# A hybrid retention layer on one NeuronCore: the first stage's modulation vectors, sums and fill rearranged

## The chip, the cores and the metric

The kernel runs on one core of a Trainium2 chip. A core has five engines that each work through their own instructions in order: TensorE (matrix products; its loads of the stationary operand are counted apart), VectorE, ScalarE, GpSimd, and SyncE, which issues transfers. Transfers run on 16 DMA engines that all issuing queues share. The metric is the device time of one execution in microseconds (us), the median of several runs.

## The reference

The layer takes 512 latent tokens `x` and 256 context tokens `ctx` of width 1024. Nine modulation vectors per token group come from one conditioning vector:

```python
mods = split((silu(c) @ w_mod + b_mod), 9)            # for x: sh1, sc1, g1, sh2, ...
mods_c = split(silu(c_ctx) @ w_mod + b_mod, 9)        # for the context
modulate(x, w, shift, scale) = rmsnorm(x, w) * (1 + scale) + shift
swiglu(x, w_in, w_out): a, b = split(x @ w_in); return (silu(a) * b) @ w_out

h  = x   + 0.5 * g1  * swiglu(modulate(x,   norm_ffn1, sh1,  sc1),  w_ffn1_in, w_ffn1_out)
hc = ctx + 0.5 * g1c * swiglu(modulate(ctx, norm_ffn1, sh1c, sc1c), w_ffn1_in, w_ffn1_out)
# then: bidirectional retention beside a convolution branch, gates, a second SwiGLU, a final RMSNorm
```

Everything is float32. The change concerns only what is needed before and during the first two column pairs of `w_ffn1_in`.

## The kernel before

Activations lie transposed: eight blocks of 128 channels (`b` = 0 to 7), each with 512 latent columns and 256 context columns in one tile `hx[b]`. A float32 product is made of three matmuls of a faster format: each operand is split into a high and a low part, and `mm3` (lines 110 to 113) issues high x high, high x low, low x high. A weight unit is loaded (line 100), its high part made on ScalarE (line 102) and its low part on VectorE (line 104). `wh` and `wl` have four buffers each; a unit holds one column block of 128 for all eight `b`.

The first stage is `start` (line 515 on), called from `ffn1`:

- `x` is loaded block by block (line 518). ScalarE squares the blocks and VectorE sums them (lines 239 to 246). `rstd_sum` adds over the channels with two-column matmuls against ones (lines 255, 256), takes a root, and `rstd_bcast` spreads the result over all partitions with one matmul (line 269).
- At the very beginning the conditioning rows `cc` are loaded into zeroed tiles, put through Silu and spread over the partitions with matmuls (line 159); ScalarE copies them out of PSUM as `ccrow` (line 521).
- `first_mods(b)` (line 167) makes scale and shift of block `b` for the latent and the context tokens. It loads 512 KB of weights for the scale and 512 KB for the shift (line 173) into tiles that later hold other operands (`th`, `tl`). The scale is eight matmuls with the two columns of `cs` held in the array and 128 weight columns streaming (line 176); the two rows that come out are copied (line 179) and transposed (line 180). The shift is a sum over products: VectorE does it for the latent tokens (line 183), GpSimd multiplies and ScalarE sums for the context tokens (lines 186, 187). `shift` (lines 194, 195) adds the two half sums and the bias.
- `norm_start` (line 505 on) makes the block's modulated input: VectorE (line 510), ScalarE's high part (511), VectorE's low part (512), ScalarE's full value (513).
- `products(n, k1)` issues the products of the first pair of column blocks (`n` = 0, `px[0]` and `px[1]`) or the second (`n` = 1) over the blocks that are ready, for the 512 latent columns. After that come the context tokens' row sums and norms, and their products for the four weights one after the other into `pc`.

`plain` in `ffn1` then takes Silu of one half times the other. `operands` (line 362) forms sums of the inputs for a saving scheme of multiplication that `chunk` uses from the fifth pair on. The third and fourth pairs follow with no such scheme. Their results, and all later ones, are accumulated in `hdram`, a DRAM tensor that is filled with `x` and `ctx` (lines 562, 563) and to which `part_sum` adds by accumulating transfers from GpSimd's queue (line 600). `mods(n)` (line 197) makes the later modulation vectors on VectorE, from weights loaded on GpSimd's queue into two `wm` buffers (line 200).

Each engine's order is made when the program is built, by a planner that takes the instructions by their place in the source but lets one go ahead when those before it on its engine aren't due yet. So the fill, which stands at the end of `start`, is issued in the first microseconds, on GpSimd's queue. A tile's buffer is reused only when all readers of its former contents are done, and the instruction that reuses it waits on its own engine.

Of the kernel before, what the change touches and what calls it, by code (L numbers as in the profile page):

```python
# [16 lines left out]
P = 128  # L17
# [37 lines left out]


# [6 lines left out]
def hybrid_layer_kernel(ctx: ExitStack, tc: tile.TileContext, a: dict, out: bass.AP):  # L63
# [62 lines left out]
    nc.sync.dma_start(cs, a["ccT"])  # L126
# [38 lines left out]
    rtags = [f"{t}{i}" for i in range(8) for t in ("th", "tl")]  # L165

    def first_mods(b):


        raw = [[t_((P, 512), F32, rtags[(4 * b + 2 * i + n) % 16]) for n in range(2)] for i in range(2)]  # L170
        for i in range(2):
            for n in range(2):
                nc.sync.dma_start(raw[i][n], a["w_mod0"][2 * b + i, :, n * 512:(n + 1) * 512])
        pm = ps()
        for k in range(KT):
            nc.tensor.matmul(pm[0:2, 0:P], cs[:, k, :], raw[0][k // 4][:, k % 4 * P:(k % 4 + 1) * P],
                             start=k == 0, stop=k == KT - 1)
        row = tmp()
        nc.vector.tensor_copy(row[0:2, 0:P], pm[0:2, 0:P])
        nc.tensor.transpose(pm[:, P:P + 2], row[0:2, 0:P], ident[0:2, 0:2])  # L180
        for n in range(2):
            c = slice(n * 512, (n + 1) * 512)
            nc.vector.scalar_tensor_tensor(tmp((P, 512), BF16), raw[1][n], 1.0, ccrow[0][:, c], ALU.mult, ALU.mult,
                                           accum_out=dots[:, b, 0, n:n + 1])
# [3 lines left out]
        nc.vector.tensor_scalar(ab1[:, 0, b, :], pm[:, P:P + 2], bm1[:, 8 + b:9 + b], vec[:, V_N1 + b:V_N1 + b + 1],  # L188
                                ALU.add, ALU.mult)
        shift(slice(b, b + 1), 0)  # L190

    def shift(bs, v):
        t = ab1[:, 1, bs, v]
        nc.vector.tensor_add(t, dots[:, bs, v, 0], dots[:, bs, v, 1])
        nc.vector.tensor_add(t, t, vec[:, V_BM + bs.start:V_BM + bs.stop])
# [232 lines left out]
    def ffn1(u):  # L428
# [7 lines left out]
        def plain(pa, pb, pc):  # L436
            s = t_((P, LA), F32, "sg", 4)
            nc.scalar.activation(s[:, xs], pa, AF.Silu)
            nc.vector.tensor_mul(s[:, xs], s[:, xs], pb)
            nc.scalar.activation(s[:, cx], pc[:, 0, :], AF.Silu)  # L440
            nc.vector.tensor_mul(s[:, cx], s[:, cx], pc[:, 1, :])
            return s
# [7 lines left out]
        for gi, (k0, nk) in enumerate(GROUPS1):  # L450
            for j in range(2 if k0 == 0 else 0, nk):
# [10 lines left out]
                keep(j, plain(pa, pb, pc))  # L462
# [52 lines left out]
    def start(u, uc):  # L515
# [7 lines left out]
        r1 = r1c = None  # L523
# [8 lines left out]
        dg = rstd_sum(acc, sq, whole)  # L532
        for b in range(KT):
            first_mods(b)
            if b == 0:
                r1 = rstd_bcast(dg)
                w += units(a["w1i"][0])
            norm_start(b, xs, r1, deriv["x1"], *u[b])
            if b == 3:
                w += units(a["w1i"][1])  # L540
            if b == 5:
                for i in range(KT):
# [597 lines left out]
```

## Time and profile before

| what | us |
|---|---|
| median of three runs | 1779.79 |
| lowest and highest run | 1775.0 and 1780.79 |
| the profiled execution, its own time | 1775.92 |
| its span, first to last instruction | 1774.1 |
| TensorE busy | 1720.5 (97%) |
| VectorE busy | 1148.9 (65%) |
| ScalarE busy | 674.4 (38%) |
| GpSimd busy | 141.9 (8%) |

A row of the page's groups names line, engine, operation, output and inputs with their shapes, then the count, the busy time in us and the mean in ns. A row of the order of time begins with start and duration in us; what stands in brackets is the idle time before it and what ended it. A row of the windows gives a stretch, its length, the busy time of TensorE, its weight loads, VectorE, ScalarE and GpSimd, the granted TensorE clock as a share of full speed, the DMA share and GB/s. Matmuls overlap, so the distance between the starts of two matmuls is their price, not the duration in the row.

### The profile page before, as it was taken

How to read it: one execution, taken by the hardware profiler on the slowest of the kernel's cores; microseconds unless marked ns; L12 is line 12 of the kernel's file. 1: busy time of each engine (PE TensorE's matmuls, PEld its weight loads, DVE VectorE, ACT ScalarE, POOL GpSimd, SP SyncE). 2: the span in 40 equal slices, each digit the busy share in tenths (PEclk: the TensorE clock that was granted, in tenths of full speed). 3: DMA queues.
4: the chain of work that ended last, by engine and by line, in shares of the span. 5: the costliest groups of instructions: out<-in, count | busy, mean ns of one | idle time of the engine just before them, and what ended most of it. 6: DMA issues, size and time to landing. Idle time of an engine off the chain costs nothing. (4 is left out here: it accounts for less than half of the span.)

```text
span 1774.1 us, 22474 instructions
## 1 busy us (share of the span) xinstructions
PE 1720.5 (97%) x8918; PEld 1495.8 (84%) x8918; DVE 1148.9 (65%) x1808; ACT 674.4 (38%) x963; POOL 141.9 (8%) x221
## 2 busy tenths in 40 slices
PE   5999999999999889999999999999999999999997
PEld 3689999998989778888888888888888988888887
DVE  5895858785767788793886679293755643333335
ACT  4643434443344532342342334233563432222222
POOL 3401020202122000010000000001100000000000
PEclk7999999999999999999999999999999999999998
DMA  9347373848585221242142125115652133333221
GB/s 342 115 135 162 119 179 105 195 164 206 188 209 190 87 83 60 68 159 72 48 155 85 58 72 178 60 48 176 198 194 97 61 118 97 99 93 101 97 84 48
DMA packets 68253, 221.95 MB, mean 125 GB/s; under 512 B 8178, under 2 KB 9202, under 8 KB 68148
## 3 DMA queue, kind: packets, MB, share of 16 engines
q1 hardware_dynamic: 45652, 146.84, 25.4%
q0 software_dynamic: 21920, 72.64, 14.9%
q8 instruction: 69, 1.13, 0.3%
q10 hardware_dynamic: 576, 1.05, 0.2%
q14 instruction: 36, 0.29, 0.0%
HBM read 192.18 MB, written 31.46 MB: 126 GB/s over the span
## 5 line engine op out<-in xcount | busy, mean ns | idle before, releaser
L102 ACT CAST wh<-wraw 128x1024 fp32r<-128x1024 f32 (+2 forms) x212 | 219.5, 1037 | 555.7 <-PE ps L112 308.7
L104 DVE TENSOR_TENSOR wl<-wraw,wh 128x1024 fp32r<-128x1024 f32 (+2 forms) x212 | 254.4, 1203 | 194.8 <-ACT wh L102 190.3
L111 PE MATMUL ps<-uh,wh 128*128 128x512 f32 (+1 forms) x924 | 332.4, 361 | 1.5 <-ACT uh L292 1.1
L113 PE MATMUL ps<-uh,wl 128*128 128x512 f32 (+1 forms) x924 | 330.6, 359 | 0.8 <-DVE wl L104 0.8
L112 PE MATMUL ps<-ul,wh 128*128 128x512 f32 (+1 forms) x832 | 297.8, 359 | 0.2
L112 PE MATMUL ps<-gx,wh 128*128 128x512 f32 (+1 forms) x544 | 204.0, 377 | 0.0
L113 PE MATMUL ps<-gx,wl 128*128 128x512 f32 (+1 forms) x544 | 204.0, 377 | 0.0
L111 PE MATMUL ps<-gx,wh 128*128 128x512 f32 (+1 forms) x544 | 203.7, 377 | 0.2 <-ACT gx L300 0.2
L111 PEld LDWEIGHTS ps<-uh,wh 128*128 128x128 f32 x924 | 174.9, 190 | 28.4 <-ACT uh L292 1.5
L113 PEld LDWEIGHTS ps<-uh,wl 128*128 128x128 f32 x924 | 175.1, 190 | 26.7 <-DVE wl L104 1.3
L696 DVE SCALAR_TENSOR_TENSOR h<-y,vec,h 128x512 f32<-128x512 f32 x240 | 179.6, 749 | 5.5
L112 PEld LDWEIGHTS ps<-ul,wh 128*128 128x128 f32 x832 | 157.8, 190 | 23.8 <-issue 0.7
L111 PE MATMUL ps<-hx,wh 128*128 128x512 f32 (+1 forms) x364 | 121.5, 336 | 5.3 <-ACT hx L300 3.8
L112 PE MATMUL ps<-hx,wh 128*128 128x512 f32 (+1 forms) x364 | 121.7, 334 | 0.7 <-DVE hx L301 0.7
L113 PE MATMUL ps<-hx,wl 128*128 128x512 f32 (+1 forms) x364 | 121.1, 333 | 0.0
L111 PEld LDWEIGHTS ps<-gx,wh 128*128 128x128 f32 x544 | 102.1, 188 | 19.2 <-ACT gx L300 0.4
L113 PEld LDWEIGHTS ps<-gx,wl 128*128 128x128 f32 x544 | 102.0, 188 | 18.7
L112 PEld LDWEIGHTS ps<-gx,wh 128*128 128x128 f32 x544 | 102.0, 188 | 18.6
L359 DVE TENSOR_TENSOR wl<-wraw,wh 128x1024 fp32r<-128x1024 f32 x54 | 66.1, 1223 | 55.6 <-ACT wh L358 55.4
L404 PE MATMUL ps<-th,wl 128*128 128x384 f32 x288 | 96.2, 334 | 0.0
L404 PE MATMUL ps<-th,wh 128*128 128x384 f32 x288 | 96.2, 334 | 0.0
L404 PE MATMUL ps<-tl,wh 128*128 128x384 f32 x288 | 96.2, 334 | 0.0
(272 smaller groups left out, 3100.5 us busy)
## 6 DMA issues: line engine op xcount, KB each, us to landing
wm<-in_w_mod POOLq DMA_DIRECT2D x56, 512.0 KB, 4.4
wraw<-in_w1i SPq DMA_DIRECT2D x44, 512.0 KB, 6.0
wraw<-in_w2i SPq DMA_DIRECT2D x44, 512.0 KB, 3.7
hdram<-sg POOLq DMA_DIRECT2D x40, 384.0 KB, 7.4
wraw<-in_w1o SPq DMA_DIRECT2D x16, 512.0 KB, 3.6
wraw<-in_w_cv SPq DMA_DIRECT2D x16, 512.0 KB, 3.8
wraw<-in_w_v SPq DMA_DIRECT2D x16, 512.0 KB, 5.7
wraw<-in_w_rg SPq DMA_DIRECT2D x16, 512.0 KB, 3.8
```

The source lines that it names most:

```text
L102: nc.scalar.copy(hi, raw)
L104: nc.vector.tensor_sub(lo, raw, f32(hi))
L111: nc.tensor.matmul(o, w[0], x[0], start=first, stop=False)
L112: nc.tensor.matmul(o, w[0], x[1], start=False, stop=False)
L113: nc.tensor.matmul(o, w[1], x[0], start=False, stop=last)
L359: nc.vector.tensor_sub(lo, src, f32(hi))
L404: nc.tensor.matmul(o, w[i][:, ws], x[k][m], start=first and k == n == 0, stop=k == 3 and n == 2, skip_group_check=True)
L696: nc.vector.scalar_tensor_tensor(o, y[:, t:t + L], vec[:, w0 + t:w0 + t + 1], o, ALU.mult, ALU.add)
```

## The change

- **Loads of the conditioning vectors.** `cs` and `cc` are loaded from ScalarE's queue. The zeroed tiles and the matmul against a first row of ones are gone; the matmul now takes one partition of `ones` and of `crow`.
- **Weights of the first modulation.** `load_mods(b)` loads them one block ahead of `first_mods(b)`. The scale weights take two `sg` tiles, or one `wm` tile in blocks 2, 3, 6 and 7; the shift weights keep a tile pair of their own for every block.
- **Scales on TensorE, the other way round.** The 128x128 weight block is held in the array and the two columns of `cs` stream, so the result is already a column per token group: no copy, no transpose.
- **Shifts.** Blocks 0 to 3 (`PE_SHIFT`) compute them in the same way on TensorE, for both token groups. In blocks 4 to 7 VectorE sums over products, for the latent tokens in `first_mods` and for the context tokens later, from the kept weights. Nothing of this is left on GpSimd or ScalarE.
- **Order in `start`.** The weights of the second pair are loaded after block 1. Products run one block closer to the norms. The context tokens are loaded after the loop; their row sums come after all products of the latent tokens; Silu and gating of the first pair come before the context norms. The context products now run with the blocks outside and the four weights inside.
- **Fill of `hdram`.** It stands after `start`, on ScalarE's queue.

```diff
     cs = cp.tile([P, KT, 2], F32, name="cs")
-    nc.sync.dma_start(cs, a["ccT"])
+    nc.scalar.dma_start(cs, a["ccT"])
...
-        nc.vector.memset(crow[v], 0.0)
-        nc.sync.dma_start(crow[v][0:1, :], a["cc"][:, v * D:(v + 1) * D])
+        nc.scalar.dma_start(crow[v][0:1, :], a["cc"][:, v * D:(v + 1) * D])
...
-            nc.tensor.matmul(pb, first, crow[v][:, c], start=True, stop=True)
+            nc.tensor.matmul(pb, ones[0:1, :], crow[v][0:1, c], start=True, stop=True)
...
+    def load_mods(b):
+        for i in range(2):
+            if i == 0 and b % 4 >= 2:
+                raw = t_((P, D), F32, "wm", 2)
+                nc.sync.dma_start(raw, a["w_mod0"][2 * b])
+                parts = [raw[:, :512], raw[:, 512:]]
+            else:
+                parts = [t_((P, 512), F32, "sg", 4) if i == 0 else t_((P, 512), F32, rtags[2 * b + n]) for n in range(2)]
+                for n in range(2):
+                    nc.sync.dma_start(parts[n], a["w_mod0"][2 * b + i, :, n * 512:(n + 1) * 512])
+            shifts[b, i] = parts
+
     def first_mods(b):
         pm = ps()
-        for k in range(KT):
-            nc.tensor.matmul(pm[0:2, 0:P], cs[:, k, :], raw[0][k // 4][:, k % 4 * P:(k % 4 + 1) * P],
-                             start=k == 0, stop=k == KT - 1)
-        row = tmp()
-        nc.vector.tensor_copy(row[0:2, 0:P], pm[0:2, 0:P])
-        nc.tensor.transpose(pm[:, P:P + 2], row[0:2, 0:P], ident[0:2, 0:2])
+        for i in range(2 if b < PE_SHIFT else 1):
+            raw = shifts[b, i]
+            for k in range(KT):
+                nc.tensor.matmul(pm[:, 2 * i:2 * i + 2], raw[k // 4][:, k % 4 * P:(k % 4 + 1) * P], cs[:, k, :],
+                                 start=k == 0, stop=k == KT - 1)
+        nc.vector.tensor_scalar(ab1[:, 0, b, :], pm[:, 0:2], bm1[:, 8 + b:9 + b], vec[:, V_N1 + b:V_N1 + b + 1],
+                                ALU.add, ALU.mult)
+        if b < PE_SHIFT:
+            nc.vector.tensor_scalar_add(ab1[:, 1, b, :], pm[:, 2:4], vec[:, V_BM + b:V_BM + b + 1])
+        else:
+            shift(b, 0)
+
+    def shift(b, v):
         for n in range(2):
             c = slice(n * 512, (n + 1) * 512)
-            nc.vector.scalar_tensor_tensor(tmp((P, 512), BF16), raw[1][n], 1.0, ccrow[0][:, c], ALU.mult, ALU.mult,
-                                           accum_out=dots[:, b, 0, n:n + 1])
-            m = tmp()
-            nc.gpsimd.tensor_mul(m, raw[1][n], ccrow[1][:, c])
-            nc.scalar.activation(m, m, AF.Copy, accum_out=dots[:, b, 1, n:n + 1])
...
+            nc.vector.scalar_tensor_tensor(tmp((P, 512), BF16), shifts[b, 1][n], 1.0, ccrow[v][:, c], ALU.mult,
+                                           ALU.mult, accum_out=dots[:, b, v, n:n + 1])
+        nc.vector.tensor_scalar(ab1[:, 1, b, v:v + 1], dots[:, b, v, 0:1], dots[:, b, v, 1:2],
+                                vec[:, V_BM + b:V_BM + b + 1], ALU.add, ALU.add)
...
+        todo_g = start(ux, uc, gate)
+        nc.scalar.dma_start(hdram[:, :, xs], a["xT"])
+        nc.scalar.dma_start(hdram[:, :, cx], a["ctxT"])
...
         dg = rstd_sum(acc, sq, whole)
+        load_mods(0)
         for b in range(KT):
+            if b == 0:
+                w += units(a["w1i"][0])
+            if b + 1 < KT:
+                load_mods(b + 1)
             first_mods(b)
             if b == 0:
                 r1 = rstd_bcast(dg)
-                w += units(a["w1i"][0])
             norm_start(b, xs, r1, deriv["x1"], *u[b])
-            if b == 3:
+            if b == 1:
                 w += units(a["w1i"][1])
...
             if b >= 1:
-                products(0, b - 1)
-            if b >= 4:
-                products(1, b - 2)
+                products(0, b)
+            if b >= 3:
+                products(1, b - 1)
+        for i in range(KT):
+            nc.sync.dma_start(hx[i][:, cx], a["ctxT"][:, i, :])
         sqc = [square_sum(accc, hx[j][:, cx], j) for j in range(KT)][-1]
...
         products(0, KT)
         products(1, KT)
-        pc = [ps((P, 2, LC)) for _ in range(2)]
-        for i in range(4):
-            proj(pc[i // 2][:, i % 2, :], w[i], uc)
+        r1c = rstd_bcast(rstd_sum(accc, sqc, wholec))
+        s = [t_((P, LA), F32, "sg", 4) for _ in range(2)]
+        gate(s[0], xs, px[0], px[1])
+        pc = [ps()[:, :LC] for _ in range(4)]
+        for b in range(KT):
+            if b >= PE_SHIFT:
+                shift(b, 1)
+            norm_start(b, cx, r1c, deriv["c1"], *uc[b])
+            for i in range(4):
+                proj(pc[i], w[i], uc, (b,))
+        gate(s[1], xs, px[2], px[3])
+        for n in range(2):
+            gate(s[n], cx, pc[2 * n], pc[2 * n + 1])
         nc.gpsimd.dma_start(rope, a["rope"])
-        nc.gpsimd.dma_start(hdram[:, :, xs], a["xT"])
-        nc.gpsimd.dma_start(hdram[:, :, cx], a["ctxT"])
```

The host-side layout of the first modulation weights changes with it: scale weights and the shift weights of blocks 0 to 3 are laid out for the array, the shift weights of blocks 4 to 7 row by row for VectorE.

More of the change, by code (lines that the diff above doesn't have):

```diff
@@ L165, in hybrid_layer_kernel @@
     rtags = [f"{t}{i}" for i in range(8) for t in ("th", "tl")]
+    shifts = {}
+    def load_mods(b):
[9 more added lines that the diff above has]
+            shifts[b, i] = parts
@@ L187, in first_mods @@
-            nc.scalar.activation(m, m, AF.Copy, accum_out=dots[:, b, 1, n:n + 1])
[L188 to L195, printed above, removed]
+            nc.vector.scalar_tensor_tensor(tmp((P, 512), BF16), shifts[b, 1][n], 1.0, ccrow[v][:, c], ALU.mult,
+                                           ALU.mult, accum_out=dots[:, b, v, n:n + 1])
@@ L434, in keep, with gate @@
             g.append((hi, lo))
[L436 to L442, printed above, removed]
+        def gate(s, c, pa, pb):
+            nc.scalar.activation(s[:, c], pa, AF.Silu)
+            nc.vector.tensor_mul(s[:, c], s[:, c], pb)
         ux, uc = part(u, xs), part(u, cx)
-        todo_g = [plain(*p) for p in start(ux, uc)]
+        todo_g = start(ux, uc, gate)
+        nc.scalar.dma_start(hdram[:, :, xs], a["xT"])
+        nc.scalar.dma_start(hdram[:, :, cx], a["ctxT"])
         t = [operands(kb) for kb in range(4)]
@@ L461, in ffn1 @@
                 proj(pc[:, 1, :], wb, uc)
-                keep(j, plain(pa, pb, pc))
+                s = t_((P, LA), F32, "sg", 4)
+                gate(s, xs, pa, pb)
+                gate(s, cx, pc[:, 0, :], pc[:, 1, :])
+                keep(j, s)
             n = 2 * nk * P
@@ L513, in norm_start, with start @@
         nc.scalar.activation(src, v, AF.Identity, bias=sh)
-    def start(u, uc):
+    def start(u, uc, gate):
         for b in range(KT):
@@ L522, in start @@
         w, px = [], [ps() for _ in range(4)]
-        r1 = r1c = None
         done = [0, 0]
@@ L536, in start @@
                 r1 = rstd_bcast(dg)
[L537 removed]
             norm_start(b, xs, r1, deriv["x1"], *u[b])
[L539 removed]
+            if b == 1:
                 w += units(a["w1i"][1])
[L541 to L543 removed]
             if b >= 1:
[L545 to L555 removed]
+                products(0, b)
[3 more added lines that the diff above has]
+            nc.sync.dma_start(hx[i][:, cx], a["ctxT"][:, i, :])
+        sqc = [square_sum(accc, hx[j][:, cx], j) for j in range(KT)][-1]
         products(0, KT)
         products(1, KT)
[L558 to L560 removed]
+        r1c = rstd_bcast(rstd_sum(accc, sqc, wholec))
[11 more added lines that the diff above has]
+            gate(s[n], cx, pc[2 * n], pc[2 * n + 1])
         nc.gpsimd.dma_start(rope, a["rope"])
[L562 to L564 removed]
+        return s
     todo = list(range(len(MOD_STEPS)))
@@ L1084, in _layout @@
     wm = w_mod[0].T.reshape(9, 8, P, D)
-    wn = w_mod[0][:, D:2 * D].reshape(KT, P, 8, P).transpose(2, 1, 0, 3).reshape(8, P, -1)
+    wn = w_mod[0][:, :2 * D].reshape(KT, P, 2, 8, P).transpose(2, 3, 1, 0, 4).reshape(2, 8, P, -1)
     wi = w_in[0]
@@ L1101, in _layout @@
         "vecs": np.concatenate(vecs, axis=1),
-        "w_mod0": np.stack([w for b in range(8) for w in (wn[b], wm[0, b])]),
+        "w_mod0": np.stack([w for b in range(8) for w in (wn[1, b], wn[0, b] if b < PE_SHIFT else wm[0, b])]),
         "w_mod": np.stack([wm[i, b] for i, b in MOD_STEPS]),
```

17 lines of the change are left out of this document (1 added, 16 removed).

## The prediction

> **What bounds the kernel now.** I read the page's row of slices first, to see where TensorE lacks work or clock, then the busy times of four long stretches, then the order of time in the first 95 us.
>
> ```profile
> span 1774.1 us, 22474 instructions
> PEclk7999999999999999999999999999999999999998
> 27.60:95.00 67.40, 59.77 (x342) 43.55 (x343) 61.62 (x139) 41.21 (x87) 27.84 (x17) 0.93 0.50 174
> 95.00:160.00 65.00, 65.00 (x372) 57.00 (x371) 51.09 (x90) 25.40 (x37) 10.46 (x15) 1.00 0.63 166
> 82.40 0.40 PE L111 MATMUL ps<-uh,wh 128*128 128x256 f32 x2
> 94.99 0.40 PE L111 MATMUL ps<-uh,wh 128*128 128x512 f32 x1
> ```
>
> The windows give, in order, TensorE, its weight loads, VectorE, ScalarE, GpSimd, the granted clock, the DMA share and GB/s. From 95 us on TensorE has no gap (65.00 of 65.00) at full clock. The change touches only the stage before that. So its worth is the shift of one landmark, which I call J: the first product of the third column pair, at 94.99, when all products of the first two pairs are done (those of the context tokens begin at 82.40). Up to J, three things are close together: TensorE 59.77 busy of 67.40, VectorE 61.62, and DMA, whose share is about 1.0 in the early windows below. I take whichever is last in each stretch.
>
> ```profile
> 3.27 0.79 POOL L562 DMA_DIRECT2D hdram<-in_xT  x1
> hx<-in_xT SPq DMA_DIRECT2D x8, 256.0 KB, 9.3
> 4.30 0.63 ACT L239 ACTIVATE acc<-hx 128x512 f32<-128x512 f32 x1 [1.57 <-DMA hx<-in_xT]
> 22.77 0.69 DVE L243 TENSOR_TENSOR t<-hx 128x512 f32<-128x512 f32 x1 [3.53 <-DMA hx<-in_xT]
> 24.12 0.59 PE L255 MATMUL ps<-ones,acc 128*128 128x2 f32 x2 [12.32 <-DVE acc L246]
> 27.62 0.58 PE L176 MATMUL ps<-th,cs 128*2 128x128 f32 x2
> 30.97 1.12 PE L269 MATMUL ps<-t,ones 128*128 128x512 f32 x2
> ```
>
> The eight blocks of x land from 4.30 to 22.77, because the fill of `hdram`, issued at 3.27, and the first weights share the bus. The row sums (16 passes, 24.12 to 27.62) and the root follow. The broadcast, from 30.97 for 1.1 us, lets the blocks be normalised.
>
> **The clock.** The granted clock changes only at multiples of 3.41 us, so I cut windows there:
>
> ```profile
> 6.84:10.25 3.41, 3.41 (x5) 1.33 (x4) 0.83 (x2) 0.63 (x1) 0.00 (x0) 1.00 1.01 381
> 10.25:13.66 3.41, 1.55 (x4) 0.38 (x2) 0.69 (x1) 0.76 (x2) 0.00 (x0) 1.00 1.04 396
> 13.66:17.08 3.42, 0.00 (x0) 0.00 (x0) 1.39 (x2) 1.13 (x2) 0.00 (x0) 1.00 1.01 372
> 23.90:27.32 3.42, 3.20 (x15) 3.20 (x16) 0.16 (x1) 0.37 (x1) 0.00 (x0) 0.50 1.03 382
> 27.32:30.73 3.41, 3.41 (x17) 2.15 (x18) 2.49 (x11) 2.77 (x5) 1.78 (x2) 0.50 1.06 359
> 30.73:34.15 3.42, 3.42 (x25) 1.98 (x23) 3.08 (x5) 0.72 (x2) 1.25 (x1) 1.00 0.91 341
> 34.15:37.56 3.41, 1.24 (x12) 0.75 (x9) 3.41 (x6) 0.00 (x0) 3.16 (x2) 1.00 1.02 347
> 37.56:40.97 3.41, 2.12 (x7) 1.35 (x8) 3.41 (x10) 2.33 (x5) 0.68 (x2) 0.50 1.04 402
> 587.11:590.52 3.41, 1.95 (x15) 1.87 (x15) 3.41 (x8) 2.27 (x5) 0.54 (x1) 1.00 0.26 97
> 589.61 0.33 PE L256 MATMUL ps<-ones,t 128*128 128x2 f32 x2
> 590.52:593.93 3.41, 0.00 (x0) 0.00 (x0) 3.34 (x11) 1.77 (x3) 0.54 (x1) 0.50 0.56 180
> 593.93:597.35 3.42, 2.96 (x12) 2.78 (x13) 3.42 (x11) 2.14 (x6) 0.00 (x0) 0.50 0.77 235
> ```
>
> The window 23.90 to 27.32 is filled with two-column passes (3.20 of 3.42), and the clock stays at 0.50. The next is filled with 128-column passes, and the clock is released at its end. A window with 1.55 busy and no two-column pass keeps the clock (10.25). One with 1.95 busy, two-column passes alone from 589.61 on, loses it (590.52). One with 1.24 loses it too (37.56). So two-column passes seem to count as nearly idle. About 0.45 of a window (1.55 of 3.41) must stream to keep the clock, and a window with 2.96 of 3.42 releases it.
>
> **The change part by part.** Prices of passes, the first and the last row of runs at full clock, then two rows at half clock, then the other engines:
>
> ```profile
> 77.70 0.38 PE L255 MATMUL ps<-ones,accc 128*128 128x2 f32 x2
> 78.62 0.49 PE L112 MATMUL ps<-ul,wh 128*128 128x512 f32 x1
> 72.25 0.39 PE L112 MATMUL ps<-ul,wh 128*128 128x512 f32 x1
> 77.47 0.39 PE L111 MATMUL ps<-uh,wh 128*128 128x512 f32 x1
> 89.11 0.28 PE L111 MATMUL ps<-uh,wh 128*128 128x256 f32 x1
> 41.44 0.63 PE L113 MATMUL ps<-uh,wl 128*128 128x512 f32 x1
> 42.29 0.63 PE L113 MATMUL ps<-uh,wl 128*128 128x512 f32 x1
> L104 DVE TENSOR_TENSOR wl<-wraw,wh 128x1024 fp32r<-128x1024 f32 x6 | 7.3, 1214 | 0.0
> L194 DVE TENSOR_TENSOR ab<-dots 128x1 f32<-128x1 f32 x8 | 6.8, 848 | 0.0
> L183 DVE SCALAR_TENSOR_TENSOR t<-th,kh 128x512 bf16<-128x512 f32 x8 | 6.0, 748 | 0.0
> L510 DVE SCALAR_TENSOR_TENSOR t<-hx,ab,ps 128x512 f32<-128x512 f32 x8 | 5.9, 735 | 0.0
> L188 DVE TENSOR_SCALAR ab<-ps,bm,vec 128x2 f32<-128x2 f32 x8 | 2.1, 268 | 0.0
> 88.83 1.05 ACT L102 CAST wh<-wraw 128x1024 fp32r<-128x1024 f32 x1
> 136.89 0.91 POOL L600 DMA_DIRECT2D hdram<-sg  x1 [0.84 <-ACT sg L599]
> 110.97 1.22 DVE L206 SCALAR_TENSOR_TENSOR t<-wm,kh 128x1024 bf16<-128x1024 f32 x1
> ```
>
> A two-column pass: 8 in 77.70 to 78.62, 0.115 us at full clock; 16 in 24.12 to 27.62, 0.219 at half. A 512-column product: 23 in 72.25 to 77.47, 0.227; at half 0.425 (41.44 to 42.29 holds two). A 256-column product: 49 in 89.11 to 94.99, 0.12.
>
> *The start.* `cs` and `cc` go to ScalarE's queue and the fill leaves GpSimd's, so x has the bus alone. The first block landed at 4.30. Seven more of 0.26 MB at 381 GB/s take 4.8, so the last is there at 9.1; with `vec` beside it I take 9.4, not 22.77. Closing the squares took 1.35 (22.77 to 24.12); ScalarE also owes two Silu rows there, so the row sums start at 11.0. Sixteen passes cost 1.8 to 3.5; I take 2.4, since the broadcast of c before them streams 512 columns and may have released the clock: 13.4.
>
> *First scales and shifts on TensorE.* A block's eight matmuls are 16 passes, now two columns wide; blocks 0 to 3 have 32, blocks 4 to 7 have 16. So 192 passes replace 128. Block 0 at half clock: 32 x 0.219 = 7.0, to 20.4; the root (at most 3.35, from 27.62 to 30.97) is hidden behind it; the broadcast ends at 21.5. Blocks 1 to 3: 96 x 0.219 = 21.0, to 42.5. Between them stand only 12 products (6 each after blocks 1 and 2), at half clock 5.1, to 47.6. After block 3 come 18 in a row: about 12 pass before a whole window streams, 5.1, then 6 x 0.227 = 1.4: 54.1. Blocks 4 to 7 at full clock: 64 x 0.115 = 7.4 and the other 66 products, 15.0: 76.5.
>
> *VectorE and GpSimd.* Gone: 16 GpSimd multiplies, 16 ScalarE sums, the row copy and transpose, and the two tiny adds per block (L194 takes 848 ns). VectorE's part from 21.5 to the last block: 8 x 2 x 0.75 for the norms, 8 x 0.27 for the scales, 4 x 0.27 at most for the first shifts, 8 half rows at 0.75 + 0.08 and 4 x 0.27 for the rest, 4 x 1.21 for `wl`: 28. It ends near 50 if fed, so TensorE at 76.5 is last and this saving shows nowhere in the sum. A 128x1 operation with three operands is not in the trace: 0.14 to 0.85, taken as L188's 0.27.
>
> *Context tokens.* The row sums now stand behind the products: 8 x 0.115 = 0.9, and of the chain to the first product (78.62 to 82.40, 3.8) I take 2.4 as bare, between nothing and all: 79.8; waits at block 7 add 0.7: 80.5. The loop issues 12 products per block, 1.44 against about 1.0 on VectorE (two norms of half L510's width), or 2.9 in blocks 4 to 7 if the context shifts are done there: between 0 and 5.8 more. I take 0, since VectorE has over 20 us free before. 96 x 0.12 = 11.5: 92.0. Blocks now run outside the four weights, so all four `wh`/`wl` pairs come free only at the end. The cast (1.05) and the subtraction (1.21) for the third pair, begun at 88.83 under cover before, lie bare with 0.3 of hand-over: 2.6. **J = 94.6**, 0.4 earlier.
>
> *Queues.* Issuing the fill costs GpSimd 0.79; on ScalarE's queue the trace has no such issue, so the two lie between nothing and three times GpSimd's price, 5 in all; I take 0, since ScalarE is idle enough after the gates. It must land before the first accumulation, at 136.89, and from near 92 it has the bus almost free. Loads of blocks 4 to 7 wait on SP for the weights of blocks 0 to 3 to be read; block 7's goes out near 47 and is used near 70, and behind it stand the context tokens and the third pair, not due before 76. GpSimd's first prefetch waits for block 6's weights, near 68; it is used at 110.97.
>
> **How the numbers follow.** The span becomes 1774.1 - 0.4 = 1773.7. The profiled execution took 1775.92, 1.8 beyond its span and 3.9 under the median, so against the median of 1779.79 I forecast **1779.4**. From the bounds above its own range is 1773 to 1785. A difference under 0.3% (5.3 us) can hardly be told from no change.
>
> **Rivals.**
> *The clock stays up* under two-column passes. For it: no window of the trace holds only such passes at full clock, so losing it there is inferred from mixed windows. Against: 587.11. Then row sums end at 12.8, block 0 at 16.5, the broadcast at 17.5; 160 x 0.115 = 18.4 and 96 x 0.227 = 21.8 give 57.7; with 4.0 to the context products, 11.5 and 2.6, 75.8; and some 4 of waits, as half of today's 7.6 (67.40 less 59.77), since VectorE (28 from 17.5, then about 20) is now close. J = 79.8: 15.2 earlier, **1764.6**.
> [...]
>
> *The clock is lost again in blocks 4 to 7* (slower). A window that holds a block's 16 passes (1.84) has 1.57 left to stream, 0.46 of it: just what kept the clock at 10.25. From about 0.1 us of waiting in such a window it falls, and a block costs 16 x 0.219 + 12 x 0.425 = 8.6 instead of 4.6. For it: TensorE waited at several blocks before. Against: VectorE runs ahead. Two blocks: 8 later than forecast, **1787.4**.
>
> *The fill isn't later.* It waits for nothing on ScalarE's queue, as on GpSimd's, where it was issued at 3.27 though it stands at the end of the stage. Sharing with it, x needs 4.2 MB of traffic instead of 2.1, 5.5 us more: **1784.9**. Against: on ScalarE it shares the in-order queue with work that waits.
> [...]
>
> **Chances.** Forecast 0.48 (0.10 of it faster, 0.33 within 0.3%, 0.05 slower), clock stays up 0.30, clock lost again 0.13, fill not later 0.09 (0.06 within, 0.03 slower). Together faster 0.40, same 0.39, slower 0.21. The range must take in the second case and part of the third: 1760 to 1786.
>
> **What would show it.** x complete before 11 us; the granted clock at 0.50 through most of blocks 0 to 3 with 0.22 us per pass; no tiny VectorE add over 0.3 us; a gap of 2 to 3 us before the third pair's first product; J between 90 and 99. I am wrong if the clock is 1.00 during two-column passes, or if TensorE waits on VectorE in the context loop.

## The result, and the profile after

The changed kernel is slower: 1795.68 us median of four runs (1793.98 to 1797.91), against 1778.16 for the kernel before (1775.0 to 1780.79) beside it. The ratio is 1.0094 with a 95% interval of 1.0073 to 1.0116, so about 17 us are lost. The profiled execution took 1795.23. Lines move by two to thirteen: the passes for scales and shifts are L186, the row sums L261 and L262, the broadcast L275, the products L113 to L115, the root on VectorE L287 to L292, `norm_start` L517 to L520.

The page of the changed kernel, its span and the granted clock in 40 slices:

```profile
span 1793.5 us, 22479 instructions
PEclk9999999999999899999999999999999999999999
```

Its windows over the stage, with length, TensorE, its weight loads, VectorE, ScalarE, GpSimd, granted clock, DMA share and GB/s:

```profile
29.48:54.94 25.46, 25.46 (x118) 25.07 (x116) 8.19 (x15) 7.43 (x10) 0.00 (x0) 1.00 0.86 306
54.94:83.53 28.59, 28.59 (x142) 24.20 (x142) 16.08 (x41) 9.86 (x18) 1.09 (x2) 1.00 0.34 117
83.53:88.97 5.44, 2.17 (x11) 1.36 (x9) 2.98 (x11) 2.22 (x5) 0.00 (x0) 0.79 0.00 2
88.97:105.11 16.14, 13.75 (x97) 13.55 (x97) 16.14 (x44) 10.89 (x22) 0.00 (x0) 0.86 0.00 1
105.11:150.00 44.89, 43.95 (x241) 38.27 (x242) 43.30 (x77) 18.11 (x24) 3.74 (x8) 0.96 0.49 157
```

The clock column misleads in the first rows. No change of the clock is recorded here before about 59 us, and up to there the views print 1.00. The spacing of the passes below shows that it was half: 0.213 us, where the kernel before had 0.219 in a window recorded at 0.50 (23.90) and 0.115 at full clock (77.70). From 54.94 on the three stages stand apart: products without a gap, then 5.44 us with only 2.17 of work, then a loop in which VectorE is busy all of 16.14.

The first 55 us in order of time, all engines, start and duration first:

```profile
10.85 0.69 DVE L249 TENSOR_TENSOR t<-hx 128x512 f32<-128x512 f32 x1 [1.35 <-DMA hx<-in_xT]
11.46 2.28 DVE L252 TENSOR_TENSOR acc<-acc,t 128x512 f32<-128x512 f32 x3
13.79 0.59 PE L261 MATMUL ps<-ones,acc 128*128 128x2 f32 x2 [1.53 <-DVE acc L252]
17.23 3.55 PE L186 MATMUL ps<-cs,sg 128*128 128x2 f32 x16
17.40 0.27 ACT L286 ACTIVATE t<-ps,epsb 128x4 f32<-128x4 f32 x1 [3.22 <-PE ps L262]
24.23 0.28 DVE L188 TENSOR_SCALAR ab<-ps,bm,vec 128x2 f32<-128x2 f32 x1 [10.50 <-PE ps L186]
24.55 0.15 DVE L287 TENSOR_SCALAR t<-ps 128x4 f32<-128x4 f32 x1
25.55 1.22 DVE L106 TENSOR_TENSOR wl<-wraw,wh 128x1024 fp32r<-128x1024 f32 x1
27.61 2.08 PE L275 MATMUL ps<-t,ones 128*128 128x512 f32 x2 [3.42 <-DVE t L268]
31.54 1.23 DVE L106 TENSOR_TENSOR wl<-wraw,wh 128x1024 fp32r<-128x1024 f32 x1 [2.85 <-ACT wh L104]
43.84 3.55 PE L186 MATMUL ps<-cs,wm 128*128 128x2 f32 x16
50.67 1.20 PE L113 MATMUL ps<-uh,wh 128*128 128x512 f32 x2
54.94 0.77 PE L114 MATMUL ps<-ul,wh 128*128 128x512 f32 x1
```

A block's 32 passes take 43.84 to 50.67, 0.213 each: half clock, with no gap between. The root is not hidden behind block 0's passes. Its VectorE part (L287) could run from 17.67 on, when ScalarE's square root (L286) was there, but stands in VectorE's order behind L188, which waits for those passes until 24.23. A `wl` of the first weight pair, 1.22 from 25.55 on, comes in between as well. So TensorE is idle for 3.42 before the broadcast.

Block 5's passes, then the end of the stage, on TensorE:

```profile
65.75 1.84 PE L186 MATMUL ps<-cs,sg 128*128 128x2 f32 x16
83.53 0.28 PE L261 MATMUL ps<-ones,accc 128*128 128x2 f32 x2
86.64 1.22 PE L275 MATMUL ps<-t,ones 128*128 128x256 f32 x2 [2.16 <-DVE t L268]
88.97 1.22 PE L113 MATMUL ps<-uh,wh 128*128 128x256 f32 x4 [1.11 <-ACT uh L518]
105.11 0.50 PE L113 MATMUL ps<-uh,wh 128*128 128x512 f32 x1 [2.39 <-ACT wh L104]
106.79 0.51 PE L113 MATMUL ps<-uh,wh 128*128 128x512 f32 x1 [0.94 <-ACT wh L104]
```

J is 105.11, 10.1 later than before. A second wait for weights follows, which the prediction did not have.

The loss does not end at J. The next rows are landmarks that both kernels pass: the first accumulation into `hdram` (at 136.89 before), the row sums of the context in the second norm, and the first product of the retention's first key. On TensorE of the kernel before:

```profile
577.77 0.38 PE L255 MATMUL ps<-ones,accc 128*128 128x2 f32 x2 [1.48 <-DVE accc L246]
633.49 0.80 PE L111 MATMUL ps<-gx,kh 128*128 128x256 f32 x2 [4.48 <-ACT gx L300]
```

On GpSimd and TensorE of the changed kernel:

```profile
149.97 0.89 POOL L610 DMA_DIRECT2D hdram<-sg  x1 [1.35 <-ACT sg L609]
593.45 0.38 PE L261 MATMUL ps<-ones,accc 128*128 128x2 f32 x2 [3.42 <-DVE accc L252]
651.82 0.80 PE L113 MATMUL ps<-gx,kh 128*128 128x256 f32 x2 [4.48 <-ACT gx L306]
```

By landmark the changed kernel is later by 10.1 (J), 13.1 (first accumulation), 15.7 (second norm), 18.3 (key product) and 19.4 (end). Three questions follow: what made J late, what the 3.0 after it are, and what the 5.2 near 600 us are.

### The profile page after: what moved, and what is told of

Its sections match the earlier page's. It is cut to its first block, busy times and chain, and to the rows that moved or that the text cites. A ratio compares the mean times of both kernels' runs of the same rounds, so it can differ in the third digit from the quotient of the medians.

```text
span 1793.5 us, 22479 instructions
## 1 busy us (share of the span) xinstructions
PE 1746.4 (97%) x8974; PEld 1529.3 (85%) x8974; DVE 1134.5 (63%) x1792; ACT 667.0 (37%) x933; POOL 112.3 (6%) x201
## 4 chain that ended last, share of the span: by engine, by line
PE 87%; DVE 5%; issue 4%; DMA 3%; ACT 1%; POOL 0%; DVEq 0%; ACTq 0%; SPq 0%; POOLq 0%
PE ps L113 24%; PE ps L114 24%; PE ps L115 24%; PE ps L410 10%; PE ps L186 2%; DMA wm<-in_w_mod 1%; DVE h L706 1%; DVE wl L106 1%; PE ps L275 0%; DVE t L212 0%; DMA gc<-hdram 0%; PE ps L262 0%; DMA hx<-in_xT 0%; PE ps L261 0%; DVE t L724 0%
## 5 line engine op out<-in xcount | busy, mean ns | idle before, releaser
L113 PE MATMUL ps<-uh,wh 128*128 128x512 f32 (+1 forms) x924 | 332.1, 364 | 5.6 <-ACT wh L104 3.3
L115 PE MATMUL ps<-uh,wl 128*128 128x512 f32 (+1 forms) x924 | 331.2, 360 | 0.0
L115 PE MATMUL ps<-gx,wl 128*128 128x512 f32 (+1 forms) x544 | 204.0, 377 | 0.0
L113 PE MATMUL ps<-gx,wh 128*128 128x512 f32 (+1 forms) x544 | 203.7, 377 | 0.2 <-ACT gx L306 0.2
L113 PEld LDWEIGHTS ps<-uh,wh 128*128 128x128 f32 x924 | 176.0, 192 | 32.6 <-ACT wh L104 4.0
L115 PEld LDWEIGHTS ps<-uh,wl 128*128 128x128 f32 x924 | 176.8, 192 | 25.7
L113 PE MATMUL ps<-hx,wh 128*128 128x512 f32 (+1 forms) x364 | 122.8, 339 | 5.0 <-ACT hx L306 3.4
L115 PE MATMUL ps<-hx,wl 128*128 128x512 f32 (+1 forms) x364 | 122.8, 338 | 0.0
L113 PEld LDWEIGHTS ps<-gx,wh 128*128 128x128 f32 x544 | 102.1, 188 | 19.1 <-ACT gx L306 0.4
L115 PEld LDWEIGHTS ps<-gx,wl 128*128 128x128 f32 x544 | 102.0, 188 | 18.8
```

The source lines that it names most:

```text
L113: nc.tensor.matmul(o, w[0], x[0], start=first, stop=False)
L115: nc.tensor.matmul(o, w[1], x[0], start=False, stop=last)
```

## The experiments

My theory was that J is late through three separate things (passes at half clock, the root behind block 0's scales, the context part), with the places of tiles behind the late loss. The rivals were loads and the fill ahead of 55 us, and for the late loss the steps of the clock, in which an idle spell would cost more or less as it happens to fall: in the changed kernel the clock was at half for 6.83 us from 86.67 on and for 3.41 from 107.15 on, in the kernel before for 6.83 from 37.56 on and for 3.41 from 491.54 on.

All runs in one table. J, the gap before the second norm's context sums and the span are read from each run's order of time. "Middle" is from the first accumulation to the first key product. Ratios are to the kernel before on the same chip.

| kernel | ratio [95%] | J | J to first accumulation | gap | middle | span |
|---|---|---|---|---|---|---|
| before | | 94.99 | 41.90 | 1.48 | 496.60 | 1774.1 |
| before_again | 1.0007 [0.9996, 1.0019] | 95.09 | 41.90 | 1.36 | 499.98 | 1778.0 |
| fill_moved | 1.0014 [0.9999, 1.0029] | 96.09 | 41.95 | 1.79 | 504.58 | 1783.7 |
| fill_late | 0.9936 [0.9911, 0.9961] | 86.89 | 41.91 | 0.67 | 498.08 | 1768.7 |
| rows_first | 1.0065 [1.0047, 1.0083] | 105.02 | 43.27 | 2.55 | 497.77 | 1787.2 |
| combo | 1.0023 [1.0007, 1.0039] | 100.04 | 42.46 | 1.26 | 497.08 | 1782.4 |
| combo_late | 0.9907 [0.9888, 0.9926] | 81.74 | 41.98 | 2.39 | 500.50 | 1765.3 |
| changed | 1.0094 [1.0073, 1.0116] | 105.11 | 44.86 | 3.42 | 501.86 | 1793.5 |
| after_again | 1.0084 [1.0060, 1.0108] | 103.88 | 44.68 | 4.03 | 501.29 | 1793.8 |
| root_first | 1.0073 [1.0058, 1.0088] | 103.17 | 44.73 | 4.24 | 501.45 | 1791.7 |
| wide | 1.0042 [1.0017, 1.0066] | 96.81 | 46.93 | 3.71 | 501.98 | 1786.7 |
| ctx_old | 1.0064 [1.0043, 1.0084] | 105.53 | 42.07 | 4.00 | 504.06 | 1792.6 |
| shift0 | 1.0072 [1.0047, 1.0098] | 102.75 | 49.00 | 4.38 | 502.41 | 1795.7 |
| after_late | 1.0081 [1.0060, 1.0102] | 102.45 | 47.76 | 4.34 | 501.93 | 1793.2 |
| wide_late | 0.9984 [0.9968, 0.9999] | 85.77 | 44.60 | 4.54 | 501.33 | 1772.0 |

In the first seven rows the reload of h begins 24 to 26 us ahead of the sums after "gap", in the other eight 17 to 18 (see *rows_first*).

### The passes: wide

```diff
-                nc.tensor.matmul(pm[:, 2 * i:2 * i + 2], raw[...], cs[:, k, :], ...)
+                nc.tensor.matmul(pm[:, P * i:P * i + P].rearrange("p (a c) -> p a c", c=2), raw[...],
+                                 cs[:, k, :].unsqueeze(1).broadcast_to([P, P // 2, 2]), ...)
...
```

> Each pass for the first scales and shifts streams the two columns of c 64 times over (128 columns) into 128 columns of PSUM, of which two are used. Theory: the clock is held by columns streamed, and a pass of 128 costs no more than one of 2 (0.11 against 0.115 us at full clock). Then the clock is released by about 24 us, 96 passes of blocks 1 to 3 save 0.104 each (10.0), block 4 and the first products some 3 to 4: J near 92, 1781 to 1784. Rival: the clock is low for another reason (weight loads bound, pauses between blocks): 1794 to 1797.

1788.46 us, ratio 1.0042, J at 96.81 instead of near 92: the theory's direction, but between its size and the rival's. In the order of time of *wide*, the broadcast:

```profile
26.95 1.22 PE L277 MATMUL ps<-t,ones 128*128 128x512 f32 x1 [3.42 <-DVE t L270]
```

Its windows, columns as above:

```profile
29.50:32.89 3.39, 3.39 (x18) 3.39 (x18) 2.00 (x3) 2.17 (x3) 0.00 (x0) 0.50 0.99 375
32.89:36.30 3.41, 3.41 (x24) 2.99 (x24) 2.71 (x5) 1.92 (x4) 0.00 (x0) 1.00 1.05 384
36.30:39.70 3.40, 3.40 (x32) 3.36 (x32) 0.79 (x2) 0.67 (x2) 0.00 (x0) 1.00 0.94 344
```

Its line L186 between 36.3 and 39.7 us, with the shortest, median and longest duration in ns and the first and last start:

```profile
L186 PE MATMUL ps<-cs,wm x14: 273/273/275, 36.1 to 37.6; 128*128 128x128 f32 x14
```

Fourteen passes of 128 columns start within 1.5 us, 0.115 each: the price of a two-column pass at full clock, and no more. The window 29.50 to 32.89, filled with them at half clock, is followed by full clock. Block 0's last eight passes show the same one gap earlier:

```profile
L186 PE MATMUL ps<-cs,tl x8: 272/274/421, 22.3 to 23.3; 128*128 128x128 f32 x8
```

The first of them still last 421 ns, the later ones 274: the clock came up near 22.7, at the end of a window that such passes filled (19.24 to 22.65, 3.41 of 3.41 busy). In the changed kernel 25.46 us without a gap, with 112 two-column passes and four products, were not followed by full clock: the products from 55.51 on came 0.43 apart up to 59.35, and 0.24 from there. So in these two kernels the clock went with the columns streamed, not with how long TensorE was busy: 3.39 us of 128-column passes were followed by full clock, 25.46 us of nearly nothing but two-column ones were not.

Nearly 5 us are missing to the expected J. The gap of 3.42 before the broadcast stands in both kernels, but here it costs more than its length: the clock, once up, was lost behind it (0.50 from 26.06 on), and block 1's passes up to 32.89 ran at half (the row 29.50), some 2 us. And a wait that the changed kernel doesn't have follows, with the clock at half from 53.4 to 56.8 behind it, some 1.7 us more:

```profile
52.70 0.50 PE L113 MATMUL ps<-uh,wh 128*128 128x512 f32 x1 [2.22 <-ACT uh L520]
```

### The passes: shift0

```diff
-PE_SHIFT = 4
+PE_SHIFT = 0
```

> No shift on TensorE: VectorE does all sixteen from the kept weights, TensorE only the first scales. Theory: the 64 two-column passes of the four shifts run at 0.213 each on the path, so 13.6 us come off, less up to 5.6 for eight more half rows in the context loop: 1782 to 1788. Rival: the stage is held by loads and VectorE, not by the passes: 1792 to 1797.

64 passes less on TensorE, and 1795.99 us, ratio 1.0072: no gain that the times show, as the rival had it. In its order of time:

```profile
34.81 1.22 PE L113 MATMUL ps<-uh,wh 128*128 128x512 f32 x2 [5.74 <-ACT uh L518]
```

Where passes are taken away, TensorE waits 5.74 for the first normalised block instead. Something else was nearly as late.

### The root: root_first

```diff
+        bias = bm1[:, 8 + b:9 + b]
+        if b == 0:
+            bias = cp.tile([P, 1], F32, name="bias0")
+            nc.vector.tensor_scalar(bias, st["dg"], 0.0, bm1[:, 8:9], ALU.mult, ALU.add)
-        nc.vector.tensor_scalar(ab1[:, 0, b, :], pm[:, 0:2], bm1[:, 8 + b:9 + b], ...)
+        nc.vector.tensor_scalar(ab1[:, 0, b, :], pm[:, 0:2], bias, ...)
...
+        st["dg"] = dg[:, dg.shape[-1] - 1:dg.shape[-1]]
```

> One tiny VectorE operation more makes the scales of block 0 wait for the root of x. Theory: the root stood behind them on VectorE and TensorE idled 3.42 us before the broadcast; now the broadcast starts within 0.5 us of block 0's last pass and all until the third pair comes 3 to 3.5 us earlier: 1792 to 1793. Rival: the first weights or the loads of block 1 are not ready earlier, or the steps of the clock swallow it: 1794.5 to 1797.

TensorE and VectorE of *root_first*:

```profile
23.68 2.05 PE L279 MATMUL ps<-t,ones 128*128 128x512 f32 x2
31.66 1.22 DVE L106 TENSOR_TENSOR wl<-wraw,wh 128x1024 fp32r<-128x1024 f32 x1 [10.06 <-ACT wh L104]
32.81 0.27 DVE L192 TENSOR_SCALAR ab<-ps,bias,vec 128x2 f32<-128x2 f32 x1
```

1793.41 us, ratio 1.0073. The broadcast now follows the passes without a gap, at 23.68 instead of 27.61, but J comes only 1.9 earlier, not 3 to 3.5. VectorE's order has the `wl` of the second weight pair ahead of block 0's scales, and it waits 10.06 for it. TensorE then waits for the first normalised block:

```profile
34.75 1.22 PE L113 MATMUL ps<-uh,wh 128*128 128x512 f32 x2 [2.40 <-ACT uh L522]
```

In the changed kernel the same `wl` stands ahead of block 0's norm (31.54). So a second chain ran close behind the passes: the second weight pair. Against the second profile of the changed kernel (*after_again*, J at 103.88) only 0.7 is left of the 1.9, so the time, just above the theory's 1792 to 1793, can hardly be told from no gain.

### Why the weights were late: after_late, fill_late, fill_moved

What SyncE's loads waited for in the changed kernel up to 60 us (waiter, total us, times, longest):

```profile
SPq L102 <- DMA hdram<-in_xT: 9.6, 1, 9.6
SPq L177 <- DMA hdram<-in_ctxT: 8.2, 1, 8.2
```

These loads read and write nothing of the fill. As the program is built, the loads of SyncE's and ScalarE's queues report their landing on eight counters in turn, and a load waits for the one that last used its counter. Moved from GpSimd's queue to ScalarE's, the fill (2 MB in one transfer) joined that turn, and the load that came to its counter next stood still until it had landed, with all later loads of SyncE behind that one. The trace bears this out in the order of issues: the part of the fill issued at 10.60, landed 15.8 later, and the first load of the second weight pair, issued at 26.54, report on the same counter, and so do the part issued at 30.47, landed 11.4 later, and the load that waited 8.2.

*after_late* holds the fill of the changed kernel back, on GpSimd's queue: one element from the scales of block 7 is written first, and the fill, which overwrites it, waits for that.

```diff
-        nc.scalar.dma_start(hdram[:, :, xs], a["xT"])
-        nc.scalar.dma_start(hdram[:, :, cx], a["ctxT"])
...
+        for c, src in ((xs, a["xT"]), (cx, a["ctxT"])):
+            nc.gpsimd.dma_start(hdram[0:1, 0, c.start:c.start + 1], ab1[0:1, 0, KT - 1, 0:1])
+            nc.gpsimd.dma_start(hdram[:, :, c], src)
```

> The changed kernel with the fill of hdram back on GpSimd's queue and held until the scales of block 7 are there. In the changed kernel SP's loads waited 9.6 and 8.2 us for the fill's landing. Theory A: TensorE is busy from 29.48 to 83.53 with passes at half clock, so these waits are covered and at most 3 us come back: 1792 to 1796. Theory B: the waits are on the path through the second weights and the norm of block 0 behind them on VectorE: 1783 to 1788.

Theory A: 1795.05, ratio 1.0081. With TensorE busy at half clock the waits are covered. J comes 2.7 earlier (1.4 against *after_again*), but the waits for the third pair's weights then fall behind it, and the first accumulation is at 150.21 against 149.97.

*fill_late* does the same in the kernel before:

```diff
+        nc.gpsimd.dma_start(hdram[0:1, 0, 0:1], ab1[0:1, 0, KT - 1, 0:1])
         nc.gpsimd.dma_start(hdram[:, :, xs], a["xT"])
+        nc.gpsimd.dma_start(hdram[0:1, 0, L:L + 1], ab1[0:1, 0, KT - 1, 0:1])
         nc.gpsimd.dma_start(hdram[:, :, cx], a["ctxT"])
```

> The kernel before with the fill of hdram alone held back until the scales of block 7 are there (a one-element write of hdram from them goes first, so the output is right in all but nothing: the fill overwrites it). Theory: 3 MB less on the bus ahead of x; x is complete by 14 to 16 instead of 22.77, row sums and block 0 follow, and J comes 6 to 9 earlier: 1771 to 1775. Rival: GpSimd's prefetch and the first weights keep the bus as full, or VectorE and the half clock bind: 1779 to 1783.

VectorE and TensorE of *fill_late*:

```profile
14.70 0.68 DVE L243 TENSOR_TENSOR t<-hx 128x512 f32<-128x512 f32 x1
86.89 0.40 PE L111 MATMUL ps<-uh,wh 128*128 128x512 f32 x1
```

1770.99 us, ratio 0.9936: 11 us faster than the kernel before. x is complete by 14.70 instead of 22.77, and J passes that gain on, 8.1. So one aim of the change pays by itself, the later fill, and the changed kernel reaches it only in part, since there the fill is issued at 10.6 and 30.5. Apart from the queue (*fill_moved*), none of its other parts was tried alone on the kernel before.

*fill_moved* only changes the queue in the kernel before, and behind the first gates in the source:

```diff
         todo_g = [plain(*p) for p in start(ux, uc)]
+        nc.scalar.dma_start(hdram[:, :, xs], a["xT"])
+        nc.scalar.dma_start(hdram[:, :, cx], a["ctxT"])
...
-        nc.gpsimd.dma_start(hdram[:, :, xs], a["xT"])
-        nc.gpsimd.dma_start(hdram[:, :, cx], a["ctxT"])
```

> The kernel before with the fill of hdram alone moved to ScalarE's queue behind the first gates. Theory: the fill held x back by more than 10 us (last block 22.77), and x by about 11 starts everything earlier; the loads of the first weights, 0.5 MB for each block on the same bus, then bound: 1766 to 1773. Rival: TensorE's half clock and VectorE's shifts bound the stage and x only waits elsewhere: 1776 to 1781.

In its order of time, the issue of the fill:

```profile
0.74 0.60 ACTq L446 DMA_DIRECT2D hdram<-in_xT  x1
```

And what SyncE's loads waited for:

```profile
SPq L520 <- DMA hdram<-in_xT: 10.2, 1, 10.2
```

The fill waits for nothing, so the planner put it first on ScalarE's queue, at 0.74. Nothing is gained: 1783.1 us against 1781.01 beside it, ratio 1.0014, nearer the rival's range than the theory's. This run doesn't test a later fill, as I had meant; it tests the queue alone, with the counters that come with it.

### The context part: ctx_old

```diff
+            if b == 5:
+                for i in range(KT):
+                    nc.sync.dma_start(hx[i][:, cx], a["ctxT"][:, i, :])
...
+        products(0, 7)
+        dgc = rstd_sum(accc, sqc, wholec)
+        products(1, 7)
+        for b in range(PE_SHIFT, KT):
+            shift(b, 1)
+        r1c = rstd_bcast(dgc)
+        for b in range(KT):
+            norm_start(b, cx, r1c, deriv["c1"], *uc[b])
+        products(0, KT)
+        products(1, KT)
+        pc = [ps((P, 2, LC)) for _ in range(2)]
+        for i in range(4):
+            proj(pc[i // 2][:, i % 2, :], w[i], uc)
```

> The changed kernel with the context part undone: context tokens loaded at block 5, their row sums between the last x products, the remaining context shifts ahead of the loop, and the context products one weight after the other. Theory: of the 13 us that the stage lost, the gaps before the context products (2.16 and 1.11), before the third pair (2.39 and 0.94) and the two spells of half clock that they set off (86.67 to 93.49, 107.15 to 110.56) are this part's: 6 to 9 us back, 1786 to 1790. Rival: VectorE owes the same shifts and norms and TensorE waits for them elsewhere: 1793 to 1797.

The first context product in its order of time:

```profile
91.46 0.80 PE L113 MATMUL ps<-uh,wh 128*128 128x256 f32 x2 [5.67 <-ACT uh L518]
```

1794.55 us, ratio 1.0064, where the theory had 1786 to 1790. Only 1 to 2.4 us come back by the first accumulation (147.60 against 149.97 and 148.56 in the changed kernel's two profiles; 42.07 from J on instead of 44.86 and 44.68). The wait for weights and the half clock after J are gone, but TensorE now waits 5.67 for VectorE, which does the eight half rows of the context shifts ahead of the norms. The rival was right for the greater part.

### The late loss: rows_first, before_again, after_again

`open_h` puts h over tiles of the first stage. In the changed kernel `sg` is allocated ahead of the half-row tiles. The first reload of h on GpSimd in the changed kernel:

```profile
576.58 0.56 POOL L619 DMA_DIRECT2D gx<-hdram  x1 [44.20 <-DVE hx L307]
```

And in *rows_first*, where the half-row tiles come first again, as in the kernel before:

```profile
561.50 1.18 POOL L620 DMA_DIRECT2D gx<-hdram  x2 [34.06 <-PE ps L411]
```

```diff
+    rows = [t_((P, 512), F32, tag) for tag in rtags]
...
-                parts = [... t_((P, 512), F32, rtags[2 * b + n]) for n in range(2)]
+                parts = [... rows[2 * b + n] for n in range(2)]
```

> Only the places of tiles change: the sixteen half-row tiles of the shifts are allocated ahead of the others, as in the kernel before. Theory: about 5 of the 19 us come late, because the first reload of h from DRAM (576.58 in the changed kernel, 552.70 before) waits for the last gate tile that lies where h goes. Then the reload goes out by about 566, the lag between 500 and 610 us does not grow by 4.7, and the time is 1790.5 to 1791.5. Rival: those 5 us come from where the idle spells fall in the 3.41 us steps of the clock: then 1794.5 to 1797.

1792.23 us, ratio 1.0065: 5 us better by the ratios and 3.5 by the medians, though the two intervals overlap. That lies between the theory's range and the rival's. The profile gives 4.1 to the middle, but the first profile of the changed kernel has the clock at half for 6.8 us there, from 503.09 on, and *rows_first* has not; that is worth up to 3.4 (half of the 6.8, an estimate) and lies well ahead of the reload. Against *after_again*, which hasn't that spell either, the middle is 3.5 shorter. To separate places from luck, both kernels were profiled once more:

> The kernel before, unchanged, in another execution. Theory: 4.6 us of the lag between 575 and 600 us are no work of the change but of where the idle spells near the second norm fall in the 3.41 us steps of the clock, and the profiled execution of the kernel before had it well there. Then this profile shows J within 1 us of 94.99 and a span 3 to 8 us longer, lost near 413, 490 and 575 to 610. Rival: the span is within 1.5 us of 1774.1 and the stretch 575 to 610 is the same; then the 4.6 belong to the change.

> The changed kernel, unchanged, in another execution. Both theories: J at 104 to 107. By the first theory the stretch near 590 to 615 differs from the first profile by 1 us or more in one direction or the other; by the rival it is the same within 0.5.

*before_again* has J and the gap before the second norm nearly unchanged, and its span is still 3.9 longer, 3.4 of it in the middle. Windows of the same place and length, *before* first:

```profile
491.54:498.36 6.82, 6.53 (x29) 5.60 (x30) 5.45 (x9) 3.42 (x7) 2.30 (x4) 0.75 0.89 246
491.67:498.50 6.83, 5.97 (x17) 5.02 (x18) 5.67 (x9) 3.15 (x6) 1.41 (x2) 0.50 0.76 262
```

The clock is at half for one step of 3.41 in the first and for two in the second, and one more such step follows at 580.42 in *before_again* alone. By the same estimate two more steps at half clock cost up to 3.4, as much as the middles differ by. The changed kernel's middle hardly moved (501.86, 501.29). So there is luck of some 4 us, and the first profile of the kernel before had it. The table shows that there is also more than luck. Seven runs with the early reload have a middle of 496.60 to 504.58, median 498.1, and a gap of 0.67 to 2.55; eight with the late one 501.29 to 504.06, median 501.9, and a gap of 3.42 to 4.54. The gaps don't overlap; the middles do, at their edges. I take 3.8 us, the distance of the medians, for the places of the tiles, as an estimate uncertain by about 2: the first profiles of the two kernels differ by 5.3 in the middle, the second ones by 1.3. Shown are the later reload and the longer gap.

### Together: wide_late, combo, combo_late

*wide_late* is *wide* with the edit of *after_late*:

> 128-column passes and the late fill together. Theory: with the passes at full clock the cover is gone and the waits for the fill are what is late (3.42 before the broadcast, 2.22 at 50.48, and the half clock after both): 6 to 10 us beyond 128-column passes alone: 1777 to 1782. Rival: nothing beyond it: 1786 to 1790.

1776.76, ratio 0.9984, 10 us beyond *wide*. J is 85.77, 11.0 earlier. So the late fill, which gains nothing that the times show beside passes at half clock, gains 10 us beside passes at full clock. Two places make that up. First, the planner has put the root ahead of block 0's scales on VectorE here, with no edit that asks for it, and the broadcast follows the passes without a gap:

```profile
17.40 0.16 DVE L289 TENSOR_SCALAR t<-ps 128x4 f32<-128x4 f32 x1 [0.60 <-ACT t L288]
23.07 1.02 PE L277 MATMUL ps<-t,ones 128*128 128x512 f32 x2
```

The first product starts at 27.41 instead of 34.25, which is 6.8 of the 11.0. It takes both the order and the late fill: *combo* below has the order with the fill early, and its first product starts at 34.24. Second, the wait of 2.22 at 52.70 in *wide* and the half clock behind it are gone, some 4.5. It hung on the fill in *wide*, on SyncE and then on ScalarE, which had the context tokens' squares ahead of the block's input:

```profile
SPq L177 <- DMA hdram<-in_ctxT: 8.0, 1, 8.0
51.62 0.42 ACT L247 ACTIVATE accc<-hx 128x256 f32<-128x256 f32 x1 [9.53 <-DMA hx<-in_ctxT]
```

How much of all this is the counters and how much the bus shared with the fill isn't separated.

*combo* joins *wide*, *root_first*, *rows_first* and *ctx_old*:

> The changed kernel with 128-column passes, the root ahead of block 0's scales, the half rows allocated first and the context part as before. If the losses found are separate they add: some 7 for the passes, 2 for the root, 6 to 9 for the context part: 1775 to 1780. If the clock or VectorE takes part of it back: 1783 to 1788.

Its first product:

```profile
34.24 0.80 PE L113 MATMUL ps<-uh,wh 128*128 128x512 f32 x1 [7.84 <-ACT uh L525]
```

1784.67, ratio 1.0023, in the rival's range: the gains don't add, as TensorE meets the second weight pair, 7.84 before the first product. *combo_late* adds the late fill and does the remaining context shifts in blocks 4 to 7:

```diff
             norm_start(b, xs, r1, deriv["x1"], *u[b])
+            if b >= PE_SHIFT:
+                shift(b, 1)
```

> All together: 128-column passes, root ahead of block 0's scales, half rows allocated first, context part as before with its remaining shifts done in blocks 4 to 7, and the late fill. Theory: the gap of 7.84 before the first product and most of the 5.61 before the context products go, with the half clock after each: 12 to 18 us better than the same without the last two, so 1767 to 1773, at or under the kernel before with the late fill alone (1771). Rival: VectorE, which now owes everything in blocks 4 to 7, becomes the bound: 1776 to 1784.

1765.09 us, ratio 0.9907 (0.9888 to 0.9926), better than both kernels. Against *fill_late* (0.9911 to 0.9961) the intervals overlap, so a gain over it isn't shown in the times, though J is 81.74 against 86.89.

## Why the prediction was wrong

The prediction gave J = 94.6 and 1779.4 us, no change within 0.3%, with 1786 as the upper end (over all its cases faster 0.40, the same 0.39, slower 0.21). J is 105.1. By its own steps:

| step | forecast, us | measured, us | off |
|---|---|---|---|
| row sums start | 11.0 | 13.79 | +2.8 |
| sixteen passes of the row sums | 2.4 | 3.4 (13.79 to 17.23) | +1.0 |
| block 0's passes | 7.0 | 7.0 (to 24.2) | 0 |
| root and broadcast behind them | 1.1 | 5.3 (to 29.48) | +4.2 |
| passes of blocks 1 to 7, x products | 55.0 | 54.05 (to 83.53) | -0.95 |
| context sums, root, waits | 4.0 | 5.44 (to 88.97) | +1.4 |
| context products | 11.5 | 13.75 (to 102.72) | +2.25 |
| bubble before the third pair | 2.6 | 2.39 (to 105.11) | -0.2 |
| J to the first accumulation | 41.9 | 44.86 | +3.0 |
| places of tiles, near 600 us | 0 | about 3.8 | +3.8 |

**The clock** was read rightly, and so were the largest terms, the passes of blocks 0 to 7 (0.213 against 0.219). *wide* agrees: full clock behind 3.39 us filled with 128-column passes. The estimate of 0.45 of a window fits one more row of the changed kernel: 1.49 us busy of the 3.41 from 499.68 on, and the clock at half from 503.09. The rival "clock stays up" fell; "clock lost again in blocks 4 to 7" fell too, as block 5's sixteen passes start at 65.75 and take 1.84.

**The step that failed first** is "the root is hidden behind it". The duration was about right (24.55 to 27.6 with a `wl` between, against 3.35 at most) and the queue was not looked at: the root's VectorE part is behind block 0's scales, which wait for the very passes that were to hide it. So "root and broadcast behind them" cost 5.3 instead of 1.1. *root_first* shows the gap gone with the order. It also shows that little is won by that alone, because the second weights are next.

**The start** was sized too small: x was complete at 10.85, not 9.4; after its last block VectorE owes its own square and three sums, 2.9 us, where I carried over 1.35 from a kernel in which x trickled in; and the clock wasn't up for the row sums (3.4 for sixteen passes).

**The context part**: I named VectorE as the risk, 0 to 5.8, and took 0. VectorE does run without a pause (16.14 of 16.14), but TensorE didn't wait for it inside the loop; the 2.25 there fit the half clock behind the chain's gap of 2.16 (0.50 from 86.67 to 93.49; 0.79 and 0.86 in the windows). The bubble was right; the second wait, 0.94, and the clock lost after it (at half from 107.15 to 110.56, some 1.7) were missed, and they make up most of the 3.0 behind J.

**"From 95 us on TensorE has no gap, so the worth is the shift of J"** failed. That is 3.0 just behind J, where *ctx_old* and both *fill* runs have 42.0, and some 3.8 near 600 us through the places of tiles, which the prediction doesn't look at.

**"The fill is not later"** came true halfway. It was issued behind x, at 10.60, which did x good, but far ahead of 92, and it held up SyncE's loads for 17.8 us. *after_late* shows that this cost nothing here that the times tell.

Together 10.1 for J, 3.0 and 3.8 make 16.9, against 17.5 between the medians. How much of the last is luck of the profiled executions stays open within about 2 us; in the second profiles of the two kernels the same three are 8.8, 2.8 and 1.3. *shift0* has the largest loss just behind J (49.00), for its waits for the third pair's weights come behind that first product, not ahead of it:

```profile
104.97 0.50 PE L113 MATMUL ps<-uh,wh 128*128 128x512 f32 x1 [1.49 <-ACT wh L104]
```

Another wait, 0.70, follows at 106.65, and the clock is at half for 6.8 us after it instead of 3.4.

## What to carry to other kernels

"Hidden behind it" needs two readings, the duration and what stands ahead of it in the order of its own engine. A gain found alone can be covered by a second chain just behind it: holding the fill back gained nothing beside two-column passes and 10 us beside 128-column ones, where the root's place came right as well, so take parts away in pairs. A new order of allocation is part of a change: what later loads are put over decides when they may start, hundreds of microseconds on. And an edit to one transfer can change the order that a planner gives to other engines, so read the order again in every run.

## What the hardware did that I had not expected

- At full clock a pass with 128 weight columns cost 0.115 us with two streamed columns (eight from 77.70 to 78.62 in the kernel before) and no more with 128 (fourteen started within 1.5 us in *wide*). The clock came up behind 3.39 us of the latter in *wide*; in the changed kernel 112 of the former, in 25.46 us without a gap, stayed at 0.213 each.
- The same program varied by some 4 us, up to 3.4 of it by the clock as estimated above: *before* and *before_again* have J at 94.99 and 95.09, and spans of 1774.1 and 1778.0, with two more steps of 3.41 at half clock in the second.
